# A two-layer decoder trunk: seven products for the second MLP matrix, woven with the first matrix, on weight sums that accumulating DMAs form

## The chip, the cores and the metric

The kernel runs on one core of one Trainium2 chip. The metric is the device time of one execution in microseconds (us), less is better. Before the change three runs gave 2387.39, 2388.78 and 2389.77 us; the median is 2388.78.

## The reference, cut to what matters

The trunk has two layers on a sequence of 1024 tokens of width 1024. Layer 0 mixes tokens by sliding-window attention beside a gated delta rule (the hybrid stage), layer 1 by a recurrent block. After each mixer comes a layer norm, then an MLP with squared ReLU, then another layer norm. The MLP is what the change touches:

```python
def sqrelu_mlp(x, w1, w2):          # x (1024, 1024), w1 (1024, 4096), w2 (4096, 1024)
    h = jax.nn.relu(x @ w1)
    return (h * h) @ w2
...
    x = layer_norm(DN_ALPHA * x + mix, ln1_g[layer], ln1_b[layer])
    x = layer_norm(DN_ALPHA * x + sqrelu_mlp(x, mlp_w1[layer], mlp_w2[layer]), ln2_g[layer], ln2_b[layer])
```

## The kernel before, in words

**Two chunks, two streams.** The 1024 tokens are cut into two chunks of 512. Each chunk is a Python generator, `stream(c)`: hybrid stage, output projection and layer norm (`mix_out`), MLP and layer norm (`mlp_ln`), four recurrent blocks (`rec_block`), output projection and layer norm, MLP and layer norm. A driver loop at the end of `trunk` decides at each step which stream (or which of the small generators in `mixers`: attention, delta rule, layer norms) puts its next instructions on the tensor engine. A stream yields nothing after a product inside a unit, `UNIT` at the end of a unit, `BLOCK` when it has to wait (for tiles of a ring, or for a flag). The stream with the lower `phase` goes first (0 in a mixer stage, 1 in the MLP of layer 0, 2 in that of layer 1), and of two in the same phase chunk 0; a stream that is in its recurrent blocks (`light`) gives the other one a turn after each unit. So the MLP of one chunk fills the gaps of the other chunk's mixer. The `Clock` class is a rough model of the engines; it only serves to choose this order. The tensor engine's instructions are then chained in the order of issue (`_pe`). On the other engines and queues a scheduler orders the instructions, and can move them ahead of earlier-written ones when their operands are there.

**Precision.** Every large product is done in three (`mm3`, L204 in the profile is the matmul call): high part by high part, high by low, low by high; high and low are float32r tiles that add up to the float32 one. Weights come by DMA in blocks of 128 x 1024 floats, 512 KB, on SP's queue into `ws` (`wblock`); the high part `wh` is a cast on ScalarE (ACT; on VectorE, DVE, every fifth time), the low part `wl = ws - wh` a subtraction on GpSimd (POOL) or DVE in turn, each for half a block, 512 columns. In the profile all of these have the line of a helper, L177; L207 is the transpose call.

**The MLP** (`mlp`). 4096 hidden rows are done in eight steps `e` of 512. In each, four blocks of the first matrix give hidden tiles of 128 rows x 512 tokens (8 x 3 = 24 matmuls of 512 columns each, `proj_fm`); ACT applies ReLU and squares, POOL squares again in full precision, DVE forms the low part. Then four blocks of the second matrix (2 output halves x 2) follow, 24 matmuls each, and for each of 4 token tiles and 2 halves DVE adds the bank to `yg`. So one step `e` is 192 matmuls, a pair of steps 384, and one chunk of one layer 1536. The last step of the last chunk of layer 1 is written so that the outputs come token tile by token tile, for the last layer norm to begin early.

**Order around the change.** Rings of SBUF tiles limit what is in flight: `g` (14 tiles of 128 x 2048), `t` (11), `s` (9), `f` (4) of 512 columns; `ws` 3 blocks; `wh` and `wl` 4 half-blocks each; PSUM has 4 banks `mm` and 4 banks `mx`. Chunk 0's MLP of layer 0 runs beside chunk 1's hybrid stage; chunk 0 then waits until chunk 1's first layer norm is written before its recurrent blocks, which alternate unit by unit with chunk 1's MLP; chunk 1's recurrent blocks wait for chunk 0's second output projection and alternate with chunk 0's MLP of layer 1; chunk 1's MLP of layer 1 comes last.

Of the kernel before, what the change touches and what calls it, by code (L numbers as in the profile page):

```python
# [17 lines left out]
P = 128  # L18
D = 1024
# [8 lines left out]
WB, HV, LG = 4, 5, 2  # L28
RINGS = dict(t=11, s=9, f=4)
# [29 lines left out]
class Clock:  # L59
    """Orders the tensor engine's work by a rough model of the engines: when each product's operands will be there."""  # L60
# [103 lines left out]
    def engine(self, eng, key):  # L164
        clk = self

        class Engine:
            def __getattr__(self, op):
                f = getattr(eng, op)

                def call(*a, **k):
# [6 lines left out]
                    if op == "dma_start":  # L178
                        clk.issue("D", outs, ins, max(0.06, aps[0].nbytes() / 360e3), 0.0, 2.0)
                        return r  # L180
# [20 lines left out]
    def matmul(self, out, lhsT, rhs, start, stop):  # L201
        n = int(np.prod(rhs.shape[1:]))
        c = 0.00042 * n * (1 if rhs.dtype == F32R else 4) if lhsT.shape[-1] > 32 else 0.046
        return self._pe(self.pe.matmul(out, lhsT, rhs, start=start, stop=stop), out, [lhsT, rhs], c, start)  # L204
# [6 lines left out]
def trunk(ctx: ExitStack, tc, I, out):  # L211
# [3 lines left out]
    DS, DA = clk.engine(nc.sync, "V"), clk.engine(nc.scalar, "V")  # L215
# [32 lines left out]
    def tl(r, dt=F32):  # L248
        return take(r, tpool.tile([P, 516], dt, tag=r, name=nm(r), bufs=RINGS[r]))

# [88 lines left out]
    def wblock(src, n=1024, hl=None):  # L339
        st = clk.tile("ws", 3, wpool.tile([P, 1024], F32, tag="ws", name=nm("ws"), bufs=3))[:, :n]  # L340
        DS.dma_start(st, src)
        m = n // 2
        if hl is None:
            hl = [clk.tile(t, WB, wpool.tile([P, 512], F32R, tag=t, name=nm(t), bufs=WB))[:, :m] for _ in range(2) for t in ("wh", "wl")]
        for i in range(2):
            h, l = hl[2 * i:2 * i + 2]
            a = st[:, i * m:(i + 1) * m]
            wcount[0] += 1
            if wcount[0] % HV == 0:
                V.tensor_copy(h, a)  # L350
            else:
                S.copy(h, a)
            if wcount[0] % LG == 0:
                G.tensor_tensor(l, a, h, ALU.subtract)
            else:
                V.tensor_tensor(l, a, h, ALU.subtract)
        return ([hl[0], hl[2]], [hl[1], hl[3]])

    def mm3(ps, lh, ll, rh, rl, start, stop):
        PE.matmul(ps, lh, rh, start=start, stop=False)  # L360
        PE.matmul(ps, lh, rl, start=False, stop=False)
        PE.matmul(ps, ll, rh, start=False, stop=stop)
# [34 lines left out]
    def load_xT(c, x, k2):  # L397
# [5 lines left out]
        else:  # L403
            st = clk.tile("ws", 3, wpool.tile([P, 1024], F32, tag="ws", name=nm("ws"), bufs=3))[:, :1024]
# [7 lines left out]
    def proj_fm(src, x, bank=None):  # L412
        wh, wl = wblock(src)
# [86 lines left out]
    def mlp(layer, yT, yg, ls, res=None):  # L500
        w1, w2 = I[f"w1_{layer}"], I[f"w2_{layer}"]
        for e in range(8):
            sh, sl = [], []
            yield from need("s", 9)
            wb, own = [], []
            if e == 7 and res is not None:
                yield from need("g", 4)
                for b in range(4):
                    t = gran(F32R)
                    own.append(t)  # L510
                    wb.append(wblock(w2[e * 4 + b], hl=[t[:, i * 512:(i + 1) * 512] for i in range(4)]))
            for f in range(4):
                ps = yield from proj_fm(w1[e * 4 + f], yT)
                h, l, r = ts("s", F32R), ts("s", F32R), ts("s")
# [4 lines left out]
                free("s", r)  # L519
                sh.append(h)  # L520
                sl.append(l)
                if e == 7 and f == 3:
                    yT.free()
# [812 lines left out]
```

## Time and profile before

| what | value |
|---|---|
| runs | 2387.39, 2388.78, 2389.77 us |
| span of the profiled execution | 2384.5 us; no time beside the span is recorded for that execution |
| mean granted TensorE clock | 0.992 |
| TensorE (PE) matmuls, busy | 12724, 2298.9 us, 96% |
| DVE, ACT, POOL busy | 56%, 38%, 35% |
| moved by DMA | 227.43 MB, 95 GB/s in the mean |

The span runs from the first to the last instruction of the profiled execution, and is 4.3 us below the median of the runs. PE's row counts a matmul as busy until its modelled end, so what it does is better read from the number of matmuls in a stretch that it fills. In names such as `mm<-g,wh` the first is the tile written, the others are read: `mm<-g,wh` and `mm<-g,wl` are products of the first MLP matrix (activations in `g`), `mm<-wh,s` and `mm<-wl,s` those of the second (hidden tiles in `s`). `ws<-w` are loads of MLP weights, `ws<-rin`, `rg`, `rout` of the recurrent block's, `ws<-hin...`, `hout` of the hybrid stage's.

### The profile page before, as it was taken

To read this page: it belongs to the slowest core of one execution; us is meant where nothing else is said; L and a number is where in the kernel's file an instruction comes from. 1 tells how busy PE (TensorE), PEld (TensorE's weight loads), DVE (VectorE), ACT (ScalarE), POOL (GpSimd) and SP (SyncE) were. 2 spreads that over 40 slices of the span, in tenths; PEclk is the share of its full clock that TensorE was granted. 3 is DMA by queue.
4 is the path that set the end of the run, shared out by engine and by line. 5 is a ranking of instruction groups with operands and counts; after the bars stand their busy time and mean duration, and the time that the engine had idled before them with its cause. 6 is when DMAs were issued, how large, how long until landed. Compare 5 with 4: busy or idle time off the path is not lost. (4 is left out here: it accounts for less than half of the span.)

```text
span 2384.5 us, 33354 instructions
## 1 busy us (share of the span) xinstructions
PE 2298.9 (96%) x12724; PEld 1841.9 (77%) x12724; DVE 1345.1 (56%) x2550; ACT 912.7 (38%) x1813; POOL 843.0 (35%) x706
## 2 busy tenths in 40 slices
PE   8889997999999999999999999999999999999997
PEld 7666775677777878778887788877887788778876
DVE  7697659565754463755664623565665543633345
ACT  5364424443333242454443322344554232322331
POOL 3342334232332243433443432343333333433341
PEclk9999998999999999999999999999999999999999
DMA  4121231122233222322333222232325222332231
GB/s 154 54 81 31 81 124 36 54 69 74 73 114 110 95 88 98 123 89 97 98 131 125 82 96 97 97 121 91 98 93 177 85 97 97 107 115 98 98 117 51
DMA packets 67487, 227.43 MB, mean 95 GB/s; under 512 B 7424, under 2 KB 7808, under 8 KB 67328
## 3 DMA queue, kind: packets, MB, share of 16 engines
q1 hardware_dynamic: 58832, 204.01, 25.9%
q10 hardware_dynamic: 8496, 21.30, 2.5%
q8 instruction: 100, 1.64, 0.3%
q14 instruction: 59, 0.48, 0.1%
HBM read 216.89 MB, written 8.39 MB: 94 GB/s over the span
## 5 line engine op out<-in xcount | busy, mean ns | idle before, releaser
L177 POOL TENSOR_TENSOR wl<-ws,wh 128x512 fp32r<-128x512 f32 (+1 forms) x372 | 497.6, 1338 | 1261.4 <-ACT wh L177 979.4
L204 PE MATMUL mm<-g,wh 128*128 128x512 f32 x2816 | 886.7, 396 | 0.5 <-DVE g L177 0.5
L177 ACT CAST wh<-ws 128x512 fp32r<-128x512 f32 (+1 forms) x595 | 365.5, 616 | 993.0 <-PE mm L204 910.1
L204 PE MATMUL mm<-wh,s 128*128 128x512 f32 x1984 | 648.2, 399 | 11.4 <-ACT s L177 5.7
L204 PEld LDWEIGHTS mm<-g,wh 128*128 128x128 f32 x2816 | 520.2, 189 | 107.2 <-issue 2.9
L204 PE MATMUL mm<-g,wl 128*128 128x512 f32 x1408 | 550.9, 391 | 5.4 <-POOL wl L177 5.4
L204 PEld LDWEIGHTS mm<-wh,s 128*128 128x128 f32 x1984 | 374.0, 189 | 102.6 <-ACT s L177 6.2
L204 PE MATMUL mm<-wl,s 128*128 128x512 f32 x992 | 391.9, 395 | 2.3 <-POOL wl L177 1.4
L177 DVE TENSOR_TENSOR wl<-ws,wh 128x512 fp32r<-128x512 f32 (+1 forms) x372 | 281.2, 756 | 188.8 <-ACT wh L177 184.4
L204 PEld LDWEIGHTS mm<-g,wl 128*128 128x128 f32 x1408 | 265.1, 188 | 64.0 <-POOL wl L177 7.1
L204 PE MATMUL mm<-wh,g 128*128 128x512 f32 (+1 forms) x768 | 235.2, 380 | 10.0 <-ACT wh L177 6.1
L177 DVE TENSOR_TENSOR s<-s,s 128x512 fp32r<-128x512 f32 x128 | 100.4, 784 | 242.9 <-POOL s L177 231.1
L204 PEld LDWEIGHTS mm<-wl,s 128*128 128x128 f32 x992 | 187.4, 189 | 43.3 <-POOL wl L177 1.8
L177 DVE TENSOR_TENSOR g<-g,mm 128x512 f32<-128x512 f32 x224 | 144.0, 680 | 130.7 <-PE mm L204 130.5
L204 PEld LDWEIGHTS mm<-wh,g 128*128 128x128 f32 x768 | 142.0, 190 | 38.7 <-ACT wh L177 6.1
L177 DVE CAST wh<-ws 128x512 fp32r<-128x512 f32 (+1 forms) x149 | 73.8, 495 | 172.6 <-PE mm L204 165.0
L177 POOL TENSOR_TENSOR s<-s 128x512 f32<-128x512 f32 x128 | 145.3, 1135 | 26.4 <-ACT s L177 26.4
L204 PE MATMUL mm<-wl,g 128*128 128x512 f32 (+1 forms) x384 | 143.7, 374 | 0.1
L177 ACT ACTIVATE s<-mm 128x512 f32<-128x512 f32 x128 | 75.9, 593 | 62.1 <-PE mm L204 61.9
L177 ACT ACTIVATE s<-s 128x512 fp32r<-128x512 f32 (+1 forms) x136 | 83.5, 614 | 19.0 <-DVE s L177 8.0
L204 PEld LDWEIGHTS mm<-wl,g 128*128 128x128 f32 x384 | 72.9, 190 | 11.9 <-DVE wl L177 0.4
L204 PE MATMUL mx<-g,wh 128*128 128x512 f32 x256 | 78.8, 389 | 0.0
(209 smaller groups left out, 2230.3 us busy)
## 6 DMA issues: line engine op xcount, KB each, us to landing
ws<-w SPq DMA_DIRECT2D x256, 512.0 KB, 3.3
ws<-hin_fm SPq DMA_DIRECT2D x32, 512.0 KB, 3.3
ws<-rin SPq DMA_DIRECT2D x32, 512.0 KB, 3.3
ws<-hout SPq DMA_DIRECT2D x16, 512.0 KB, 3.4
ws<-rout SPq DMA_DIRECT2D x16, 512.0 KB, 3.4
t<-ln ACTq DMA_DIRECT2D x28, 256.0 KB, 4.2
ws<-hin_q SPq DMA_DIRECT2D x8, 512.0 KB, 3.2
g<-x ACTq DMA_DIRECT2D x8, 512.0 KB, 5.0
```

Of the source, the lines that this page charges most:

```text
L177: r = f(*a, **k)
L204: return self._pe(self.pe.matmul(out, lhsT, rhs, start=start, stop=stop), out, [lhsT, rhs], c, start)
```

## The change

**Seven products.** A pair of steps (1024 hidden rows, index `j` = 0 to 3) multiplies a 512 x 1024 by a 1024 x 1024 matrix. The change cuts both into quarters, `a11 .. a22` (256 tokens x 512 hidden rows) and `b11 .. b22` (512 x 512), and forms the four output quarters from seven products instead of eight (the Strassen-Winograd form). Each product is 2 weight blocks of 12 matmuls, a unit each, so a pair takes 168 matmuls for the second matrix instead of 192. Four of the products need sums of weight quarters (`t1` to `t4`), and three need sums of hidden quarters, which DVE forms in place, 128 x 1024 at a time (four such instructions a pair). The hidden tiles are kept in float32 in `g` tiles, and each unit makes its own split of them (an ACT copy and a DVE subtraction of 512 columns) into two tiles of the ring `s` or `t`. Products accumulate on in a bank after DVE has added it to `yg` (`more=True` in `mm3`): two banks `mm` and two `mx` stay taken. DVE adds a bank to `yg` 14 times a pair instead of 16. In this path every `wl` is formed on DVE (`pool=False`).

**Where it is used.** `mlp` goes through plain steps (`straight`) until a check at an even step succeeds: chunk 1, or chunk 0 once chunk 1's output projection of the same layer is done (`op`). From there on `first(j)` makes the hidden tiles of a pair, and `weave` alternates one unit of `first(j + 1)` (24 matmuls) with two units of `seven(j)` (12 each); the last `seven` of a chunk has no partner. The last chunk of layer 1 starts with one plain step and closes with the old token-by-token step (`ends`, `finish`), so that it has three pairs.

**Weight sums.** `w2_sums` writes `t1` to `t4` of 2 layers x 4 pairs to DRAM. For each pair: four copies of 1 MB on SP's queue, 4 us of the model's clock apart; seven accumulating DMAs of 1 MB on POOL's queue in rows of 8 KB, 5 us apart; 8 us more, then the pair counts as summed, and `seven` may begin. A scheduling edge keeps each one behind the tensor engine's last instruction at that point. It starts when chunk 1's hybrid stage is over.

**Order.** Chunk 1's first layer norm in each layer waits until chunk 0 has used up the first matrix of that layer (`m7`); chunk 0's second layer norm of layer 0 waits for chunk 1's `m7`; a recurrent block `b` of chunk 1 waits for block `b` of chunk 0, no longer for its output projection. Chunk 1's recurrent blocks use ring `s`.

**Tiles.** Ring `s` 10 instead of 9, its square helper in a ring of its own (`r`, 2); `wh`, `wl` 3 whole blocks each instead of 4 half-blocks; the split works on a whole block, 1024 columns, at a time.

```diff
-WB, HV, LG = 4, 5, 2
-RINGS = dict(t=11, s=9, f=4)
+WB, WS, HV, LG = 3, 3, 5, 2
+RINGS = dict(t=11, s=10, f=4)
...
+    def split(h, l, x, key):
+        wcount[0] += 1
+        (V.tensor_copy if wcount[0] % HV == 0 else S.copy)(h, x)
+        (G if key else V).tensor_tensor(l, x, h, ALU.subtract)
...
+    def w2_sums():
...
+        for layer, j in ((i, j) for i in range(2) for j in range(4)):
+            for k, (first, *_) in SUMS.items():
+                behind(DS.dma_start(rows(tsum[layer][j][k]), rows(w2_quarter(layer, j, first))))
+                t = clk.now + 4.0
+                yield lambda: t
+            for i in range(1, 4):
+                for k, v in SUMS.items():
+                    if i < len(v):
+                        t = clk.now + 5.0
+                        yield lambda: t
+                        behind(DG.dma_start(rows(tsum[layer][j][k]), rows(w2_quarter(layer, j, v[i])), accum_op=ALU.add,
+                                            max_dma_last_dim=8192))
+            summed.add((layer, j))
+            t = clk.now + 8.0
+            yield lambda: t
...
+        def hidden(f, z):
+            ps = yield from proj_fm(w1[f], yT, mm_ps, False)
+            used()
+            S.activation(z, ps, AF.Relu)
+            S.activation(z, z, AF.Square)
+            yield UNIT
+
+        def seven(j, g, done):
...
+            yield from wait(lambda: (layer, j) in summed)
+            A = {f"a{r + 1}{q + 1}": v4(g[q])[:, :, r * 256:(r + 1) * 256] for q in range(2) for r in range(2)}
+            bank = {}
+            for i, (a, b, acc, out, sign, last) in enumerate((
+                    ("a12", "b21", "R", (0, 0), 1, False), ("a11", "b11", "X", (0, 0), 1, True),
+                    ("a21", "t1", "R", (1, 1), 1, False), ("a21", "t2", "X", (0, 1), -1, False),
+                    ("a12", "b22", "R", (0, 1), 1, True), ("a21", "t3", "X", (1, 1), -1, True),
+                    ("a22", "t4", "X", (1, 0), 1, True))):
...
+                for p in range(2):
+                    yield from wait(lambda: either(2))
+                    ring = either(2)
+                    ah, al = ts(ring, F32R), ts(ring, F32R)
...
+                    S.copy(ah2, x)
+                    V.tensor_tensor(al2, x, ah2, ALU.subtract)
+                    wh, wl = wblock(w2_quarter(layer, j, b)[p * P:(p + 1) * P], pool=False)
+                    for k in range(2):
+                        for t in range(2):
+                            mm3(bank[acc][t], ah2[:, k, t * P:(t + 1) * P], al2[:, k, t * P:(t + 1) * P], wh[k], wl[k],
+                                start and p + k == 0, p + k == 2, not start)
+                            if p + k == 2:
+                                accumulate(bank[acc][t], 2 * out[0] + t, out[1], sign, done and last)
...
+        if res is not None:
+            yield from straight(6, False)
+        while e < 8 and not ((c == 1 or sts[1].get("op", -1) >= layer) and rings["g"] >= 2 and e % 2 == 0):
+            yield from straight(e, e == 7)
+            e += 1
+        if e < 8:
+            n = 3 if res is not None else 4
+            yield from first(e // 2)
+            for j in range(e // 2, n):
+                nxt = first(j + 1) if j + 1 < n else ends() if res is not None else None
+                yield from weave(nxt, seven(j, hids.pop(j), j == 3), 2)
+        if res is not None:
+            yield from finish()
```

290 lines of the change are left out of this document (183 added, 107 removed).

## The prediction, made before the changed kernel ran

> **What bounds the kernel now.** I read the page's busy shares first, then the busy time by stretches, then single matmuls in the timeline, then the groups of the other engines, and last the queue of weight loads.
>
> ```profile
> span 2384.5 us, 33354 instructions
> PE 2298.9 (96%) x12724; PEld 1841.9 (77%) x12724; DVE 1345.1 (56%) x2550; ACT 912.7 (38%) x1813; POOL 843.0 (35%) x706
> ```
>
> ```profile
> 500.00:2325.00 1825.00, 1799.15 (x8811) 1460.78 (x8811) 942.21 (x1537) 682.79 (x1194) 654.87 (x531) 1.00 0.31 102
> ```
>
> The second fence is the stretch from the middle of the hybrid stage to the last hidden blocks (columns: us, then PE, PEld, DVE, ACT, POOL, then granted clock, DMA share, GB/s). PE idles 1825 - 1799 = 26 us there and the clock is 1.00: matmuls are what it waits for, and a matmul less is time less, as long as nothing new stops PE. The other engines have room in the mean: DVE, the fullest, is busy 942 of 1825 us.
>
> **Part 1: fewer matmuls.** What one costs, from the timeline of PE (start, length, names):
>
> ```profile
> 2252.14 0.62 PE L204 MATMUL mm<-g,wh 128*128 128x512 f32 x2
> ...
> 2258.94 0.62 PE L204 MATMUL mm<-g,wh 128*128 128x512 f32 x2
> ...
> 2260.08 0.64 PE L204 MATMUL mm<-wh,s 128*128 128x512 f32 x2
> ...
> 2280.25 0.63 PE L204 MATMUL mm<-wh,s 128*128 128x512 f32 x2
> ```
>
> The first two rows are 10 groups of three apart (30 products of the first matrix in 6.80 us, 227 ns each), the last two 29 groups (87 of the second matrix in 20.17 us, 231.8 ns each). A pair of steps does 168 instead of 192: 24 x 0.2318 = 5.56 us saved per pair.
>
> A page has a price for this too: the Trainium skill, "TensorE: Matmul & The Clock Gate", section "Wait — 56ns, not 53.3ns?", gives 215.7 ns from start to start for 512 columns once warm, by which a pair would save 5.18 us; the row above is the kernel's own and stands.
>
> How many pairs? Chunk 1 has four in layer 0 and three in layer 1 whatever happens. Chunk 0 has those that begin after chunk 1's output projection. From SP's queue:
>
> ```profile
> 350.97 120.62 SPq L177 DMA_DIRECT2D ws<-w  x11
> ...
> 661.85 93.06 SPq L177 DMA_DIRECT2D ws<-w  x14
> 761.25 40.03 SPq L177 DMA_DIRECT2D ws<-hout  x8
> 806.39 165.26 SPq L177 DMA_DIRECT2D ws<-w  x30
> ...
> 1555.88 0.33 SPq L177 DMA_DIRECT2D ws<-rin  x1
> ...
> 1807.83 5.56 SPq L177 DMA_DIRECT2D ws<-w  x2
> 1818.67 41.01 SPq L177 DMA_DIRECT2D ws<-rout  x8
> ```
>
> Before `hout` of chunk 1 (761 us), 40 blocks `ws<-w` were issued (the first 11 and the last 14 shown): eight a step, so five steps. If the order up to there stays, chunk 0 does step 5 plainly, and the check at step 6 succeeds: one pair. In layer 1, 28 blocks (3.5 steps) go between the first `rin` of chunk 1 and its `rout` (first and last shown). In the new order some of chunk 1's recurrent units pass under chunk 0's projection and norm, so I put chunk 0 at step 2 to 3 when chunk 1's projection begins; the check at step 4 succeeds: two pairs. Sum 1 + 4 + 2 + 3 = 10 pairs, 240 matmuls, **-55.6 us**; from 7 pairs (-39) to 11 (-61).
>
> **Part 2: the other engines under the seven products.** One unit of `seven` is 12 matmuls, 12 x 0.2318 = 2.78 us of PE. What it asks of DVE goes by these rows:
>
> ```profile
> 2225.48 0.68 DVE L177 TENSOR_TENSOR wl<-ws,wh 128x512 fp32r<-128x512 f32 x1
> 2226.09 1.87 DVE L177 TENSOR_TENSOR g<-g,mm 128x512 f32<-128x512 f32 x3
> 2229.73 0.43 DVE L177 CAST wh<-ws 128x512 fp32r<-128x512 f32 x1 [1.77 <-PE mm L204]
> ```
>
> Back to back, a 512-column DVE instruction takes 2226.09 - 2225.48 = 0.61 us. A unit has: a hidden split 0.61, `wl` of a whole block 1.22, one bank added 0.61, a fourteenth of the four 1024-column sums of hidden quarters 4 x 1.22 / 14 = 0.35, and a fifth of a cast of 2 x 0.43 us, 0.17: 2.96 us. Alone, `seven` is thus held by DVE by 0.18 us a unit, 2.5 us over its 14 units, 39 us of PE. Woven, two units go with a hidden block of 24 x 0.227 = 5.44 us of PE and 1.4 us of DVE: 7.3 of 11.0 us, no bound. `seven` stands alone at the end of chunk 0's part in each layer and of chunk 1's in layer 0, where a layer norm also wants DVE: **+7**, from 0 (DVE works ahead in the tiles of two rings) to 20. Removing POOL's 8 squares a pair and its `wl` is worth nothing: the weights are split ahead of PE. ACT has 0.62 + 2 x 0.62 = 1.9 us a unit by this row, under 2.78:
>
> ```profile
> L177 ACT CAST wh<-ws 128x512 fp32r<-128x512 f32 x582 | 360.5, 620 | 991.1 <-PE mm L204 908.4 <-PE mx L204 51.8 <-issue 20.7
> ```
>
> **Part 3: layer norms that change their cover.** Chunk 1's first layer norm now waits until chunk 0 has used its first matrix. Rows of ACT, PE and DVE around it today:
>
> ```profile
> 756.18 0.96 ACTq L177 DMA_DIRECT2D t<-ln  x2
> ```
>
> ```profile
> 774.97 0.60 PE L207 MATMUL mx<-csb,t 128*128 128x128 f32 x4
> ```
>
> ```profile
> 825.76 0.39 PE L204 MATMUL mm<-wh,g 128*128 128x512 f32 x1
> ```
>
> ```profile
> 829.71 0.70 DVE L177 SCALAR_TENSOR_TENSOR g<-g,lnw,t 128x512 f32<-128x512 f32 x1
> ...
> 859.71 0.68 DVE L177 TENSOR_TENSOR g<-mx,g 128x512 fp32r<-128x512 f32 x1
> ```
>
> From the first normalisation to the last split it is 30 us. PE ends the output projection at 826; step 5 is 4 x 5.44 + 4 x 5.56 = 44 us, and `first(3)` 8 x 5.44 = 43.5: the flag comes at about 913. The sums begin when the hybrid stage is over, at 775 (second row), and a pair takes 4 x 4 + 7 x 5 + 8 = 59 us, with about 0.5 more at each of 12 steps 65; pair 3, chunk 0's only one, is summed at 775 + 4 x 65 = 1035. So between 913 and the norm's end PE has nothing to put under it. The first row shows that work goes out ahead of its place in the program (the norm's loads go 74 us before the norm). If its arithmetic does too, it is over before 913, and only transposes and the last splits stand open: +3. If not, +30. I take **+3**.
>
> Chunk 0's recurrent blocks now run against chunk 1's last `seven` and then against chunk 1's own second norm, in place of a long MLP. `seven` has 14 units; alternating they last 14 x (5.44 + 2.78) = 115 us, then the norm takes 30, and chunk 0 has 20 units, about 6 left, 33 us: just enough. **+5**, from 0 to 30.
>
> **Part 4: the sums' transfers.** There is no accumulating DMA in this trace. The price of 1 MB:
>
> ```profile
> q1 hardware_dynamic: 58832, 204.01, 25.9%
> ```
>
> ```profile
> ws<-w SPq DMA_DIRECT2D x256, 512.0 KB, 3.3
> ```
>
> ```profile
> 1044.00:1165.00 121.00, 118.90 (x520) 97.08 (x519) 73.33 (x92) 62.21 (x101) 46.36 (x44) 1.00 0.29 96
> ```
>
> 204 MB took 25.9% of 16 engines' 2384.5 us, so 330 GB/s at full use, and 1.05 MB is 3.2 us of all engines. An accumulation costs between that (as a copy) and three times that, 9.6 us (source and destination read, then written, each at that rate). I take 5: nearer to the copy's row, since reading and writing already overlap in a copy. A pair then needs 4 x 3.2 + 7 x 5 = 48 us of the engines, and weights at the 29% of the last row take 19 of each 65: 67, full but in step. Weights land in 3.3 us today. Woven, 22 blocks in 82 us leave three block buffers 11.2 us, less 2.5 for the split: 8.7 us to land; a copy of 3.2 to 6.4 us ahead of a load in the same SP queue makes 6.5 to 9.7. So PE waits at few of them: **+8**, from 0 to 30. POOL issues seven transfers in 65 us; SP's issue of a load takes 0.33 us, a POOL issue was never seen here; POOL is 65% idle and splits weights ahead of PE, so even several us each, and a wait of t4's third accumulation for its second (5.5 us later), cost nothing until POOL falls a block of 5.5 us behind. Whole-block splits and three block buffers of `wh` in place of two change the hybrid stage by 0, plus or minus 5.
>
> Sum: -55.6 + 7 + 3 + 5 + 8 = -32.6. The span would be 2352; with the 4.3 us between span and median of the runs, 2388.8 - 32.6 = **2356 us**.
>
> **The rivals.** (a) **The sums come late** (slower). PE's order is fixed when the kernel is built, by the clock of a model; chunk 0's pair 3 stands in it at 1035 whether its sums are there or not. The last of the sums, t4, is used 12 units (33 us) in, which with the 8 us of grace gives about 36 us for all. At 6.4 us an accumulation, a pair needs 12.8 + 45 + 19 = 77 of 65 us, 12 late a pair, 48 after four: 12 us of standstill. At 8.5 us it is 26 a pair, 104 after four: 68 us, and 2388.8 - 32.6 + 68 = **2424**. It decides from 33 us of standstill on, about 7.3 us an accumulation. For: the accumulation must read its destination too. Against: DMA engines are 69% idle now. The Trainium skill, "DMA: Bandwidth & Descriptors", says in "Rules for kernel authors" that an accumulating DMA reads its destination and writes it later, and in "Bandwidth" that 1 MB issued from GpSimd takes 6.15 us; estimated by that for copies and sums alike, the fourth pair would be 4 x (68 + 19 - 65) = 88 us late and the time 2408. No trace here shows it.
>
> (b) **Cover lost**: the arithmetic of the norm is not done ahead, and the recurrent stages of two chunks against each other leave PE idle at both their ends: 27 + 25 us on top, 2388.8 - 32.6 + 52 = **2408**. For: 30 us of norm, and no long MLP beside chunk 0's recurrent blocks. Against: the early loads.
>
> (c) **Fewer pairs**: chunk 0's check fails in both layers, 7 pairs, -39 + 20: **2370**.
>
> (d) **Nothing gained**: short units make DVE and the weight loads the bound where `seven` runs, 0.4 us in each of 14 x 10 units takes back 56, all of part 1 in place of parts 2 to 4: **2388**. Against: DVE at 7.3 of 11 us when woven.
>
> **How the numbers follow.** Forecast 0.52, (c) 0.14, (d) 0.10, (a) 0.13, (b) 0.11. What a measurement can tell from no change is about 0.2%, 5 us. Of (d) I give 0.08 to no change; (a) and (b) are slower, with a little of (d): 0.25; the rest, 0.67, is faster. The range: all ten pairs and hardly a stall is 2388.8 - 54 = 2335; at the other end it takes in (b) at 2408 and the milder (a): 2410. The forecast's own range is 2335 to 2372.
>
> **What would show it.** Right: 12724 - 240 = 12484 matmuls or near, PE idle between 500 us and the last hidden blocks below 60 us, weight loads of 4 to 8 us while the sums run, and `seven` alone with DVE as the releaser. Wrong: PE waiting on a DMA of `t1` to `t4` near 1035 (a); 20 to 30 us of idle PE before chunk 1's first hidden block or after chunk 0's last recurrent block (b); about 12556 matmuls (c).

## The result, and the profile after

The changed kernel takes 2443.55 us (median of four runs, 2442.12 to 2446.47), the kernel before 2388.12 us beside it (2387.39 to 2389.77): a ratio of 1.0232, 95% interval 1.0220 to 1.0244. It is 55 us slower, and 34 us beyond the upper end of the range.

From the page after (the execution took 2442.44 us): the span, the busy times, DMA engines' busy tenths in 40 slices of 61 us, SP's and POOL's DMA queues with packets, MB and share of 16 engines' time, and POOL's issues of accumulating transfers. In the changed kernel the matmul call is L206, the helper L178 and the transpose call L210.

```profile
span 2440.7 us, 32068 instructions
...
PE 2264.4 (93%) x12460; PEld 1808.9 (74%) x12460; DVE 1551.8 (64%) x2537; ACT 1003.5 (41%) x1723; POOL 550.9 (23%) x399
...
DMA  4220231122235899979887862422443443534452
...
q1 hardware_dynamic: 69360, 272.17, 32.3%
q0 software_dynamic: 8064, 58.72, 11.9%
...
L178 POOL DMA_DIRECT2D t<-w x56 | 45.9, 866 | 373.5 <-DMA t<-w 359.7
...
t<-w POOLq DMA_DIRECT2D x56, 1024.0 KB, 12.0
```

PE does 12460 matmuls, 264 fewer: eleven pairs, one more than forecast, 264 x 0.2318 = 61 us less work. It spends more time all the same. The third row shows where to look: from the 14th slice to the 23rd the DMA engines are busy to seven to nine tenths, where two to four are usual elsewhere. The last rows are the new transfers: 56 accumulations took 11.9% of 16 engines' 2440.7 us, 290 us, so **5.2 us of all engines each** (forecast 5), but each lands 12.0 us after its issue, and POOL stands 360 us waiting for earlier ones before it may issue the next.

The stretch that the prediction's second fence showed, up to the last hidden blocks, which come some 60 us later now, and four parts of it (us; PE, PEld, DVE, ACT, POOL; clock, DMA share, GB/s), after:

```profile
500.00:2385.00 1885.00, 1770.71 (x8564) 1431.46 (x8563) 1148.47 (x1556) 777.89 (x1150) 374.37 (x260) 0.97 0.54 166
...
767.00:1000.00 233.00, 223.69 (x983) 183.34 (x982) 108.21 (x132) 75.16 (x103) 47.92 (x40) 0.98 0.89 250
1000.00:1320.00 320.00, 277.94 (x1110) 216.11 (x1109) 186.88 (x234) 114.64 (x155) 28.62 (x30) 0.94 0.88 257
1320.00:1420.00 100.00, 92.61 (x409) 74.25 (x408) 80.63 (x88) 54.70 (x79) 42.10 (x31) 0.98 0.83 236
1420.00:1700.00 280.00, 239.69 (x1049) 194.93 (x1048) 208.50 (x253) 159.03 (x228) 101.77 (x67) 0.94 0.33 109
```

Three of these parts before:

```profile
767.00:1000.00 233.00, 229.44 (x1033) 187.13 (x1032) 126.89 (x207) 75.84 (x127) 88.04 (x67) 1.00 0.30 100
1000.00:1320.00 320.00, 316.70 (x1384) 259.03 (x1383) 178.18 (x237) 143.61 (x232) 115.29 (x103) 1.00 0.33 109
...
1420.00:1700.00 280.00, 275.45 (x1216) 224.84 (x1215) 138.40 (x209) 112.62 (x183) 99.98 (x81) 1.00 0.31 101
```

PE's idle time in the long stretch has grown from 26 to 114 us. The count of matmuls tells it best: from 1000 to 1320 us, where the units of `seven` are woven with the hidden blocks, PE does 1110 instead of 1384, 274 x 0.2318 = 64 us behind; from 1420 to 1700, where the transfers are over (DMA share 0.33), 167 behind, 39 us; from 767 to 1000, with just as much DMA traffic, only 50, 12 us. DVE, ACT and POOL are not near their limits: DVE, the fullest of them, has 187 of 320 us.

What the loads did from 1000 to 1320, after (count, KB each, median us from issue to landing):

```profile
t<-w POOLq DMA_DIRECT2D x25, 1024.0 KB, 12.1
ws<-w SPq DMA_DIRECT2D x43, 512.0 KB, 7.3
ws<-t SPq DMA_DIRECT2D x28, 512.0 KB, 8.9
t<-w SPq DMA_DIRECT2D x14, 13.4
```

Weight loads, of `w` and of the sums `t` alike, land in 7 to 9 us instead of 3.3. The view of waits in the same stretch shows who stood for them:

```profile
ACT wh L178 <- DMA ws<-t: 63.6, 13, 9.2
ACT wh L178 <- DMA ws<-w: 62.8, 15, 9.0
...
PE mm L206 <- ACT wh L178: 19.8, 11, 5.8
PE mm L206 <- DVE wl L178: 13.9, 18, 2.7
```

(In this view: us in total, times, longest wait.) ACT's cast waits 126 us for loads, PE for the cast and the low part 34. PE names ACT and DVE as releasers, but they are held up themselves; one step further back stands the DMA.

PE's waits do not make up the whole loss. Its idle time from 1000 to 1320 is 320 - 278 = 42 us, and the granted clock there is 0.94 instead of 1.00. Right after a wait the matmuls themselves are slower, as two rows of PE's timeline behind a wait of 2.07 us for `wh` show:

```profile
1107.90 1.05 PE L206 MATMUL mm<-wh,s 128*128 128x512 f32 x2
...
1109.18 1.05 PE L206 MATMUL mm<-wh,s 128*128 128x512 f32 x2
```

A group of three takes 1.28 us here, where the prediction's rows have 0.68 to 0.70 (3 x 0.227 and 3 x 0.2318). So a late load costs more than the wait that it causes.

And one wait after the transfers, in PE's timeline:

```profile
1471.42 2.82 PE L210 MATMUL mx<-csb,g 128*128 128x128 f32 x12 [23.75 <-DVE g L178]
```

These are the first transposes of chunk 1's second layer norm of layer 0. PE stood still for 23.75 us, and the units that follow in the fixed order were behind these transposes.

### The profile page after: what moved, and what is told of

The parts are those of the page before. It is cut to its first block, busy times and chain, and to the rows that moved or that the text cites. A ratio compares the mean times of both kernels' runs of the same rounds, so it can differ in the third digit from the quotient of the medians.

```text
span 2440.7 us, 32068 instructions
## 1 busy us (share of the span) xinstructions
PE 2264.4 (93%) x12460; PEld 1808.9 (74%) x12460; DVE 1551.8 (64%) x2537; ACT 1003.5 (41%) x1723; POOL 550.9 (23%) x399
## 3 DMA queue, kind: packets, MB, share of 16 engines
q0 software_dynamic: 8064, 58.72, 11.9%
## 4 chain that ended last, share of the span: by engine, by line
PE 63%; DVE 20%; DMA 7%; ACT 5%; issue 2%; POOL 0%; ACTq 0%; DVEq 0%; POOLq 0%
PE mm L206 50%; PE mx L206 11%; DVE g L178 7%; DMA ws<-w 6%; DVE wl L178 3%; DVE t L178 3%; DVE s L178 2%; ACT wh L178 1%; DVE lnw L178 1%; DVE f L178 1%; PE mx L210 1%; DVE hsc L178 1%; DMA ws<-t 1%; ACT t L178 1%; ACT g L178 1%
## 5 line engine op out<-in xcount | busy, mean ns | idle before, releaser
L206 PE MATMUL mm<-g,wh 128*128 128x512 f32 x2816 | 891.9, 398 | 10.9 <-ACT wh L178 7.2
L178 ACT CAST wh<-ws 128x1024 fp32r<-128x1024 f32 (+1 forms) x350 | 364.8, 1042 | 789.3 <-PE mm L206 595.1
L178 DVE TENSOR_TENSOR wl<-ws,wh 128x1024 fp32r<-128x1024 f32 (+1 forms) x335 | 420.6, 1257 | 393.0 <-ACT wh L178 388.9
L206 PEld LDWEIGHTS mm<-g,wh 128*128 128x128 f32 x2816 | 523.4, 190 | 122.9 <-ACT wh L178 9.6
L206 PE MATMUL mm<-g,wl 128*128 128x512 f32 x1408 | 554.1, 394 | 11.9 <-DVE wl L178 11.9
L178 POOL TENSOR_TENSOR wl<-ws,wh 128x1024 fp32r<-128x1024 f32 (+1 forms) x103 | 252.2, 2448 | 831.8 <-ACT wh L178 461.3
L206 PE MATMUL mm<-wh,s 128*128 128x512 f32 x1216 | 410.6, 405 | 26.7 <-ACT wh L178 12.6
L206 PEld LDWEIGHTS mm<-g,wl 128*128 128x128 f32 x1408 | 266.6, 189 | 73.5 <-DVE wl L178 16.7
L206 PEld LDWEIGHTS mm<-wh,s 128*128 128x128 f32 x1216 | 235.1, 193 | 82.4 <-ACT wh L178 15.7
L206 PE MATMUL mm<-wl,s 128*128 128x512 f32 x608 | 243.7, 401 | 9.3 <-DVE wl L178 9.3
L206 PE MATMUL mm<-wh,g 128*128 128x512 f32 (+1 forms) x768 | 231.6, 379 | 9.2 <-ACT wh L178 6.3
L206 PE MATMUL mx<-wh,s 128*128 128x512 f32 x528 | 171.0, 392 | 3.2 <-DVE s L178 1.7
L206 PEld LDWEIGHTS mm<-wh,g 128*128 128x128 f32 x768 | 142.5, 191 | 35.7 <-ACT wh L178 6.3
L206 PEld LDWEIGHTS mm<-wl,s 128*128 128x128 f32 x608 | 117.8, 194 | 36.0 <-DVE wl L178 13.0
L206 PE MATMUL mm<-wl,g 128*128 128x512 f32 (+1 forms) x384 | 143.9, 375 | 0.3 <-DVE wl L178 0.3
L178 ACT CAST s<-g 128x512 fp32r<-128x512 f32 x158 | 95.5, 620 | 99.3 <-PE mm L206 50.6
L178 DVE TENSOR_TENSOR s<-g,s 128x512 fp32r<-128x512 f32 x158 | 110.4, 713 | 36.0 <-ACT s L178 35.9
L178 POOL DMA_DIRECT2D t<-w x56 | 45.9, 866 | 373.5 <-DMA t<-w 359.7
L178 DVE CAST wh<-ws 128x1024 fp32r<-128x1024 f32 x88 | 62.3, 708 | 94.8 <-PE mm L206 60.2
L206 PEld LDWEIGHTS mx<-wh,s 128*128 128x128 f32 x528 | 99.0, 188 | 25.1 <-DVE s L178 3.0
L178 DVE TENSOR_TENSOR g<-g,mm 128x512 f32<-128x512 f32 x140 | 92.0, 681 | 28.5 <-PE mm L206 28.3
L206 PE MATMUL mx<-wl,s 128*128 128x512 f32 x264 | 103.3, 391 | 3.5 <-DVE wl L178 3.5
```

The costliest lines, as they stand in the source:

```text
L178: r = f(*a, **k)
L206: ins = self.pe.matmul(out, lhsT, rhs, start=start, stop=stop, skip_group_check=fresh)
```

## The experiments

Two theories stood against each other at first. **T**: the transfers of the sums take the bandwidth from the weight loads. **C**: cover is lost, above all under that norm. The further ones, with letters of their own, are in the expectations, which are quoted as they were put on record. The kernel before ran beside every group, with medians of 2387.46 to 2388.29 us. All kernels are the changed one with the edit shown, unless said otherwise. Runs 9 and 11 to 18 also carry a guard of two lines in the model's clock, which skips an entry that is no longer queued.

### 1. No traffic for the sums

```diff
-behind(DS.dma_start(rows(tsum[layer][j][k]), rows(w2_quarter(layer, j, first))))
-behind(DG.dma_start(rows(tsum[layer][j][k]), rows(w2_quarter(layer, j, v[i])), accum_op=ALU.add, ...))
+clk.issue("D", [...], [...], 2.9, 0.0, 2.0)     # both: the model's entry alone, so PE's order stays
...
-return tsum[layer][j][q] if q in SUMS else ...
+return ... the first quarter of the sum, as it lies in w2
```

> The changed kernel without the 32 copies and 56 accumulating DMAs: no sum is formed, each of t1 to t4 is read from the raw quarter that it would start from, so four of the seven products multiply by the wrong weights. The order of the tensor engine's instructions is the same, instruction for instruction. Theory T (the sums' transfers fill the DMA engines, 0.88 to 0.89 busy from 767 to 1320 us, and the weight loads land in 8 to 11 us and up to 24 instead of 3.3): the 80 us that PE loses in matmuls between 767 and 1420 us come back, 2443 - 75 = 2368 us, between 2355 and 2380, with the loss of 39 us between 1420 and 1700 still there. Rival D (short units, whole-block splits and all low parts on DVE make DVE late, and the transfers only look guilty): under 15 us come back, 2430. Rival L (the loss between 1420 and 1700 is itself an effect of the delay before it, since the order was planned by a clock that knows no delay): both come back, about 2330.

2373.12 us (2373.01 to 2376.14), ratio 0.9942 [0.9927, 0.9956]. Its windows and its wait:

```profile
767.00:1000.00 233.00, 227.48 (x1006) 186.64 (x1005) 109.57 (x136) 78.25 (x107) 33.39 (x18) 0.99 0.28 97
1000.00:1320.00 320.00, 309.25 (x1361) 253.35 (x1361) 234.81 (x288) 148.76 (x204) 27.37 (x17) 0.99 0.42 145
1320.00:1420.00 100.00, 74.52 (x333) 60.41 (x332) 82.34 (x103) 53.70 (x77) 40.32 (x29) 0.88 0.33 116
1420.00:1700.00 280.00, 265.54 (x1152) 216.86 (x1151) 187.25 (x218) 155.53 (x221) 98.92 (x61) 0.97 0.32 110
```

```profile
PE mx L210 <- DVE g L178: 34.3, 12, 24.1
```

With the same order of PE's work, the transfers cost 2443.6 - 2373.1 = 70 us, as T had it. The matmuls tell where: against this run the changed kernel is 23 behind from 767 to 1000, 251 from 1000 to 1320 and 27 from 1320 to 1700; these 301 x 0.2318 are 70 us. Of the 58 us in the middle part some 31 are idle time of PE (42 against 11) and the other 27 slower matmuls. The 24 us under the norm (last number of the last row) stay, so they are no effect of the traffic, C does not explain the 70, and rival L of the expectation is out. From 1320 to 1700 this run does 1485 matmuls against 1647 before, some 38 us behind, though it has no transfers: that part of the loss belongs to the order of the work. The rows say something more: without sums the woven stretch asks for 0.42 of the DMA engines by itself, the plain one before it for 0.28.

### 2. Plain products, the rest of the change kept

```diff
-            spawn(w2_sums())
...
-        while e < 8 and not ((c == 1 or sts[1].get("op", -1) >= layer) and ...):
+        while e < (8 if res is None else 6):
...
```

> The changed kernel with all products of the second matrix done plainly, eight and not seven, and no sums: what is left of the change is the order of the two chunks, the rings, the whole-block splits and three block buffers. Against the run without the sums' traffic it has 264 matmuls more, 61 us. If order and splits cost nothing of themselves: 2388. Theory H (the new order of the chunks leaves the layer norm of chunk 1 and the recurrent blocks uncovered, some 39 us): 2425. Rival S (it is the DVE work of seven beside chunk 0's recurrent blocks that opens that gap, since DVE was 90% busy there): 2390 to 2400.

2421.87 us (2418.75 to 2424.45), 1.0142 [1.0127, 1.0157]. That is close to theory H's 2425. So the seven products alone are worth 2421.9 - 2373.1 = 49 us of the 61 that their matmuls come to, and the order of the chunks, the rings and the buffers cost 34 us against before.

### 3. Layer 1's sums later, and 4. all sums earlier

```diff
+            if layer:                                      # run 3
+                yield from wait(lambda: "m7" in sts[1])
...
-        if c == 1:                                         # run 4
+        if c == 0:
             spawn(w2_sums())
```

> The sums of layer 0 as they are, those of layer 1 only from the moment when chunk 1 has used up the first matrix of layer 0, about 1320 us, into the recurrent blocks, whose own traffic is low. Theory T: from 1100 to 1320 us the loads land early again, about 45 us back there, and a little lost after 1320: 2400, between 2390 and 2410. Rival D: 2435 to 2445.

> The sums begin when chunk 0's hybrid stage is over, about 290 us, instead of chunk 1's: they are through at about 930. The engines for DMA are 20 to 30% busy there, and weights are read in blocks of 5.4 us or more, not of 2.78. Theory T: of 80 us some 50 come back; but POOL waits for one accumulation before it issues the next on the same sum, and in the hybrid stage POOL has work that the delta rule's chain needs, which costs 10 to 25: 2400 to 2420. Rival D: 2440, or slower by POOL's waits.

Run 3: 2404.7 us (2398.48 to 2406.77), 1.0074 [1.0057, 1.0090], as T had it: half of the transfers, moved out of the woven stretch, give back 39 us. Run 4: **2373.81 us** (2372.02 to 2375.42), 0.9941 [0.9926, 0.9956], below every range that was expected (the 10 to 25 us of POOL's waits did not come), and 14 us faster than the kernel before. It moves the same bytes as the changed kernel and, in an order of PE's work of its own, takes no longer than run 1 without transfers. Its windows:

```profile
500.00:767.00 267.00, 262.84 (x2062) 207.38 (x2061) 148.59 (x307) 93.70 (x208) 103.03 (x83) 1.00 0.90 242
...
1000.00:1320.00 320.00, 315.97 (x1405) 260.37 (x1405) 209.14 (x237) 149.70 (x208) 19.85 (x12) 1.00 0.40 138
```

Before, the first of these stretches had:

```profile
500.00:767.00 267.00, 263.88 (x2064) 208.06 (x2064) 151.26 (x340) 98.67 (x238) 84.54 (x75) 1.00 0.27 90
```

At 0.90 of the DMA engines PE does 2062 matmuls where it did 2064 at 0.27: beside the hybrid stage the transfers are free. The granted clock is 1.00 here, so the transfers do not lower it by themselves; in the changed kernel it is low where PE had waited. A full DMA system is no harm by itself. It harms where the loads that share it are needed at once. The changed kernel shows the same from 767 to 1000 us:

```profile
ws<-w SPq DMA_DIRECT2D x34, 512.0 KB, 8.1
```

The loads land as late there as in the woven stretch, and only 5 us are lost: a plain block lasts PE 24 matmuls, 5.5 us, a block of `seven` 2.8.

### 5. Cover for the norm, and 6. low parts on POOL again (both on run 4's kernel)

```diff
-        yield from mlp_ln(0, c, s, "t", False)             # run 5
+        yield from mlp_ln(0, c, s, "ts"[c], False)
...
-                    wh, wl = wblock(..., pool=False)       # run 6, and proj_fm in hidden
+                    wh, wl = wblock(...)
```

> The sums early as in the run before, and chunk 1's layer norm after the MLP of layer 0 takes its four tiles of gains and offsets from ring s, not t. Theory R: the 24 us in which PE waits for that norm at about 1375 us come from ring t: the norm holds four of its eleven tiles, chunk 0's last recurrent block needs them, is blocked, and so four hidden blocks of 5.4 us and the gates' 5.5 that could lie under the norm are planned behind it. Then 15 to 25 us come back: 2352, between 2347 and 2362. Rival V: DVE is too busy there for any order to help: 2368 to 2376.

> The sums early, and the low parts of the weights formed on POOL and DVE in turn in the woven part too, as in the plain steps, instead of on DVE alone (the order of the tensor engine's instructions stays, instruction for instruction). Theory V (where seven meets recurrent blocks and norms, DVE at 80 to 95% is the bound): 5 to 15 us come back, 2362. Rival: these waits are for single results, not for DVE's throughput, and POOL's 2.4 us for a block come later than DVE's 1.2: 2370 to 2378.

Both missed. Run 5: 2384.57 us (2378.62 to 2390.49), 0.9988 [0.9976, 0.9999], 11 slower than run 4. The 24 us are gone (such waits come to 9 in all, the longest 1.9), and others have come:

```profile
PE mx L206 <- DVE t L178: 19.4, 12, 10.2
PE mx L206 <- ACT t L178: 13.8, 5, 6.6
PE mm L206 <- ACT r L178: 10.8, 4, 5.9
...
PE mx L210 <- issue: 9.0, 2, 8.5
```

Its 12484 matmuls are ten pairs: the ring changed the order, and chunk 0 began its seven products one pair later. 5.6 us are that pair; the other 5 may be that the work put under the norm was needed elsewhere, but they are no more than small edits move this kernel by (runs 13 to 18). Run 6: 2383.9 us (2381.5 to 2387.6), 0.9979 [0.9970, 0.9988], with DVE relieved by 87 us in all (1475.8 busy instead of 1562.4) and 10 us slower. Theory V's 2362 is out. A low part of a block takes POOL 2.4 us and DVE 1.3 (means on the changed kernel's page), so a relief of DVE came together with later low parts, and the run does not weigh the two apart.

### 7. Copies on ACT's queue, and 8. copies without accumulations

```diff
-behind(DS.dma_start(rows(tsum...                           # run 7
+behind(DA.dma_start(rows(tsum...
...
-behind(DG.dma_start(..., accum_op=ALU.add, ...))           # run 8
+clk.issue("D", [...], [...], 2.9, 0.0, 2.0)
```

> The changed kernel with the 32 copies issued from ACT's queue instead of SP's; nothing else. Theory Q (loads are late because a copy of 1 MB stands in front of them in SP's own queue): over 25 of the 70 us that the traffic costs come back, 2400 to 2418. Theory F (the 16 engines are full and the loads share them, whichever queue the copies are in): under 10 us, 2433 to 2446.

> The changed kernel with the 32 copies and without the 56 accumulations: t1 to t4 stay what the copy put there, so four of the seven products multiply by the wrong weights. The order on PE is the same. The accumulations took 11.9% of 16 engines' span, 290 us or 5.2 us each, the copies about 2 to 3 each. Theory F: nearly all of the 70 us come back, 2375 to 2385. Theory Q: about half, 2405.

Run 7: 2452.25 us (2449.78 to 2453.34), 1.0264 [1.0249, 1.0279]: 9 slower than the changed kernel, outside both ranges. That a copy stands ahead of a load in SP's queue is not the cost. The Trainium skill, "DMA: Bandwidth & Descriptors", section "Issuing engines are not separate DMA queues", says that all of them run on the same 16 engines whoever starts them; this run agrees, with a DMA share of 0.86 from 1000 to 1320 us where the changed kernel had 0.88. Run 8: 2378.46 us (2375.63 to 2381.94), 0.9957 [0.9942, 0.9973]: of the 70 us the 32 copies cost 5, the 56 accumulations 65. Its woven stretch:

```profile
1000.00:1320.00 320.00, 309.09 (x1363) 252.81 (x1362) 235.46 (x289) 149.37 (x205) 27.95 (x17) 0.99 0.57 205
```

The copies add 0.15 to the 0.42 of run 1, and PE does 1363 matmuls, as without them (1361). Whether the accumulations do their harm by their share alone or also by their kind or the queue that they come from is open: no run filled the engines as far with plain copies.

### 9. The old order, with seven products in layer 1 only, and 10. the old order with plain products

```diff
-"s" if c == 0 else "t", s, st[c]["t"], lambda: c == 0 or "m7" in sts[0])
+"s" if c == 0 else "t", s, st[c]["t"], lambda: True)
+st[c]["ln1"] = True
...
+        if c == 0:
+            yield from wait(lambda: "ln1" in st[1])
+        else:
+            yield from wait(lambda: "rec" in st[0])
...
-            yield from wait(lambda: c == 0 or sts[0].get("rb", 0) > b)
-                yield from rec_block(c, b, s["x"], hT, s, "ts"[c])
+                yield from rec_block(c, b, s["x"], hT, s, "t")
...
-                if c == 0:
-                    yield from wait(lambda: "m7" in sts[1])
...
+        while e < 8 and not (layer and ...        # run 9; layer 1's sums alone, 15 us apart
...                                               # run 10: plain products, as in run 2
```

> The order of the two chunks as it was before the change (chunk 0's recurrent blocks beside chunk 1's MLP, chunk 1's beside chunk 0's), rings and whole-block splits as changed, and seven products only in layer 1, where the rings have room: four pairs, 96 matmuls, 22 us less. The sums of layer 1 alone, begun after chunk 1's hybrid stage, accumulations 15 us apart. Theory H (what is left of the loss without traffic, some 34 to 46 us, lies in the new order, which puts the two recurrent stages against each other with no long MLP beside them): 2370, between 2362 and 2378, faster than before by about 0.8%. Rival D (it lies in the splits and in seven itself): 2385 or more.

> The changed kernel's rings, whole-block splits and three block buffers of high and low parts with the old order of the chunks, plain products only and no sums: 12724 matmuls as before. Theory H: within 5 us of before, 2383 to 2393, and so the new order costs 2422 minus this, about 34 us. Rival D: 2400 or more, the splits cost it.

Run 10 (run 2 with the old order): 2405.97 us (2403.8 to 2408.52), 1.0074 [1.0058, 1.0089], so of the 34 us of run 2 the new order is 16, and 18 stay in a kernel that has no sums, no seven products and the old order. Theory H, which had put all of it on the order, missed here and by 3 us in run 9. Run 9, four pairs in layer 1 beside it: 2380.87 us (2378.98 to 2383.75), 0.9972 [0.9961, 0.9984], 25 under run 10; its 96 fewer matmuls come to 22. So here, with the sums spread out, the seven products seem worth all that they save. The two kernels differ in PE's order, though, and runs 13 and 14 will show plain products in the old order at 2390, with one other edit each, only 9 above run 9.

### 11 and 12. Half-block splits again, in run 10's kernel and in run 4's

```diff
+        m = x.shape[1] // 2
+        for i in range(2):
+            hi, li, xi = (z[:, i * m:(i + 1) * m] for z in (h, l, x))
...
```

> As the run with the old order and plain products, but each weight block split in two halves of 512 columns again, cast and low part, on three whole-block buffers. Theory G (the 18 us that rings and splits cost come from instructions of 1024 columns standing in front of short ones of the norms and chains on ACT, DVE and POOL): 2386 to 2394. Rival (they come from the rings and from what the planner then does around the norms): 2400 to 2410.

> The changed kernel with the sums begun early, which ran at 2374, and each weight block split in two halves again. Theory G: 10 to 18 us less, 2356 to 2364, the best of all. Rival: 2370 to 2380, since the woven part has more instructions on DVE.

2411.92 us (2409.55 to 2414.98), 1.0096 [1.0081, 1.0112], and 2375.81 us (2373.24 to 2377.82), 0.9949 [0.9936, 0.9961]: 6 slower than run 10, the same as run 4. Theory G is out: the splits' size is not the 18 us.

### 13 to 16. The rings and the buffers

```diff
-either = lambda n: next((r for r in "st" if rings[r] >= n), None)   # run 13, on run 10's kernel
+either = lambda n: "s" if rings["s"] >= n else None
...
-WB, WS, HV, LG = 3, 3, 5, 2                                         # run 14, on run 10's; run 16, on run 4's
+WB, WS, HV, LG = 2, 3, 5, 2
...
-r = clk.tile("r", 2, ...)                                           # run 15: 13 and 14 and this
+r = ts("s")                                                         # with ring s = 9
```

> The kernel with the old order of the chunks and plain products only (2406.0 us, 18 above before), with one edit: a plain step takes its hidden tiles from ring s alone, as before the change, and no longer from ring t where s is short. Theory R (the +18 is rings: the MLP's steps take eight of the eleven t tiles that the recurrent blocks beside it need): about 2392, and the matrix engine's waits for DVE's additions (38 us in that kernel, 3 us before) mostly gone. Theory W (the +18 is split work done too far ahead: three whole blocks of wh and wl in place of two, so that DVE makes the low parts of later blocks first and is late with the additions that free the banks): 2404 to 2408, no change. Theory S (spread over several small edits): 2398 to 2404.

> The same kernel (2406.0 us) with one other edit: two whole blocks of wh and wl instead of three, the size of the buffers before the change. Theory W: about 2393, and the waits for DVE's additions mostly gone. Theory R: 2406 or slower, since the splits have less room ahead. Theory S: 2398 to 2404.

> The same kernel (2406.0 us) with both of these edits and the square helper back in ring s (9 tiles). What is left of the change then are whole-block splits (no loss by themselves: halves were 6 us slower), the layout of the second matrix in quarters and the code that makes all eight tiles of a step at its start. Theories R, W and S alike: within 5 us of before, 2385 to 2393. If it stays at 2400 or above, none of the rings and buffers is the cause.

> The changed kernel with the weight sums begun after chunk 0's hybrid stage (2373.8 us), with two whole blocks of wh and wl instead of three. Theory W, if it holds where the seven products are too: 2358 to 2368. Theory R: 2374 to 2385, slower, since a unit of the seven products uses up a block in 2.8 us and two blocks leave less ahead.

Run 13: 2389.62 us (2386.01 to 2393.52), 1.0007 [0.9998, 1.0017]. Run 14: 2390.37 us (2384.46 to 2392.35), 1.0008 [0.9998, 1.0018]. Run 15: 2386.97 us (2384.73 to 2390.39), 0.9999 [0.9989, 1.0008]. Either edit alone gives the 16 us back, so they are not a sum of two costs, and neither theory is right as it was put. The largest wait of PE for DVE in run 10 and in run 13:

```profile
PE mm L206 <- DVE g L178: 38.3, 12, 8.7
```

```profile
PE mx L212 <- DVE g L180: 25.7, 10, 5.8
...
PE mm L208 <- DVE g L180: 6.2, 4, 2.1
```

(The lines of runs 13 to 16 stand two further down; L212 there is the transpose call.) In run 10 matmuls wait for DVE to clear their bank into `yg`; in run 13 that wait has shrunk, and transposes wait more. In run 14, as fast as run 13, it is still 29.7 us:

```profile
PE mm L208 <- DVE g L180: 29.7, 13, 7.9
```

So this wait is not the 16 us either. Run 16: 2416.19 us (2415.39 to 2422.08), 1.0123 [1.0108, 1.0138]: with two split blocks the kernel of run 4 loses 42 us, more than either theory gave it. PE's largest wait for low parts there:

```profile
PE mm L208 <- DVE wl L180: 25.0, 26, 5.6
```

In run 4 this wait was 5.1 us. A unit of `seven` uses up a block in 2.8 us, and the seven products need the third buffer: 42 us are well above what the other edits of buffers did.

### 17 and 18. Ring t kept out of the plain steps, in run 4's kernel and in run 2's

```diff
-            yield from wait(lambda: either(8))
-            ring = either(8)
+            yield from need("s", 8)
+            ring = "s"
```

> The changed kernel with the weight sums begun after chunk 0's hybrid stage (2373.8 us), and a plain step that takes its tiles from ring s alone (a unit of the seven products may still use both rings). If the 16 us that this edit gave back in the old order are a cost of ring t as such, they come back here too: about 2358. If they belong to the order that the planner made of that kernel only, there is no reason for a gain: 2368 to 2382, of either sign, since only the few plain steps of chunk 0 and the last chunk's first step are touched.

> The kernel with the new order and plain products only (2421.9 us), with the same edit. If ring t costs 16 us whatever the order: 2406, and the new order costs 16 by itself. If the two overlap, so that the new order already pays for what ring t costs, 2415 to 2422. If the planner's orders scatter by this much under any small edit, anything from 2400 to 2430.

2380.24 us (2377.61 to 2382.6), 0.9968 [0.9954, 0.9982], and 2415.25 us (2412.9 to 2419.47), 1.0115 [1.0100, 1.0130]: one 6 us slower, the other 7 faster than its partner. The edit that gave 16 us in the old order has no fixed price. Run 18 fits two of its theories, that of the overlap and that of the scatter. Taken together, small edits of rings and buffers reorder the planned work, and the times here lie some 6 to 18 us apart without a cause that these runs name.

## Why the prediction was wrong, point by point

**The sum.** By the medians, from before: +34 (run 2: order, rings, buffers), -49 (seven products, run 2 to run 1), +70 (transfers, run 1 to the change) make the 55 us.

**Part 4, the step that failed.** It said of a pair "67, full but in step" and "So PE waits at few of them: **+8**, from 0 to 30". It was 70. The price of an accumulation came out, 5.2 us of all engines for 5. No row had spoken for 5 between the bounds of 3.2 and 9.6, so that was luck; an accumulation of 7.3 us, from which rival (a) was to decide, was not needed. What failed is the room, in two terms. I took the weights' own share, 29%, from a stretch of plain steps; the woven stretch asks for 0.42 (run 1). The prediction had the numbers for it: it counts 22 blocks in 82 us when woven, and at its 3.2 us for 1 MB, 1.6 a block, these are 35 of 82 us, 0.43. And a pair does not come every 65 us: in run 8, where nothing slows PE much, the first copies of the pairs are 73 us apart in the mean (eight pairs, first copies at 770 to 1279 us). With both put right a pair needs 48 + 0.42 x 73 = 79 of 73 us.

The engines were not full all the time either: in stretches of 20 us from 1000 to 1320 their share went from 0.54 to 1.07, for 0.88 in the mean. The transfers come in bursts; between two pairs POOL issues none for some 30 us (1049 to 1082, say). An estimate from three rows: sums that find room take 0.90 - 0.27 = 0.63 of the engines (run 4, 500 to 767), with the 0.42 that is 1.05, and at 0.88 everything would take 1.05 / 0.88 = 1.19 times as long; 1361 / 1.19 = 1144 matmuls from 1000 to 1320, measured 1110. The plain stretch asks for 0.28 + 0.63 = 0.91, and lost 23 matmuls to run 1, against 251. So the same transfers cost 5 us in one stretch and 58 in the next. The other side of the sum, the time for a load to land, was forecast at 6.5 to 9.7 us against 8.7 available; the medians were 7.3 and 8.9. Forecast and bound lay within one another, which should have been read as a coin's toss and not as "in step". Whether too little share or too little time for each load is the better account of the harm, these runs do not tell. Nor was it a price to be paid once: each transfer is held behind a PE instruction and each accumulation behind earlier ones, so sums and PE slowed down together, and by the same measure the pairs came 82 us apart.

**Rival (a)** had the resource right and the place wrong: no fourth pair stood still for its `t4`; weight loads of all kinds in the woven stretch were late. In the whole run only POOL waits for a `t<-w` (360 us, before its next accumulation); SP's queue never holds a load of `t` for an unfinished sum. Its 2424 was reached and passed.

**Part 1.** Right, and one pair better: 264 matmuls for 240, -61 for -55.6. Rival (c), seven pairs, is out.

**Part 2.** +7 forecast, 61 - 49 = 12 measured. The named cause, DVE's throughput in `seven` alone, is not shown: relieving DVE did not help (run 6), but made its low parts later. Rival (d), all of part 1 taken back, is out.

**Part 3.** For the first norm, +3: run 1 does 27 matmuls fewer than before from 767 to 1000, 6 us. For chunk 0's recurrent blocks against chunk 1's second norm, +5 of a range 0 to 30: there stands the wait of 24 us. I had counted six units left at that point, "just enough"; as I read the planned order, chunk 0's next recurrent block had no tiles left in ring t to start on, and with tiles from ring s for the norm the wait is indeed gone (run 5). The time did not gain, so the ring is not all of it. In all, the new order costs 2421.9 - 2406.0 = 16 us by one pair of kernels and 2415.3 - 2389.6 = 26 by another, for the 8 forecast. That is rival (b), in part; since 16 to 26 us are hardly more than the scatter of the orders, the size is uncertain.

**Part 4's "0, plus or minus 5"** for splits and buffers: 18 us in run 10, nothing in runs 13 to 15. Shown is that undoing either ring t for plain steps or the third block gives it back; that this is a scatter of the planned orders, and no mechanism of its own, is what runs 17 and 18 suggest. It is not settled: no run here holds PE's order fixed and changes a ring.

**What would have been right.** With the sums begun after chunk 0's hybrid stage the same change gives 2373.8 us, 14 faster than before: -61 + 12 + 34 and next to nothing for the transfers. That lies inside the forecast range, but the -61 and the 46 against it are not the forecast's -55.6 and 15.

## What to carry to other kernels

Price a background transfer in the stretch where it will run, by the share of the DMA engines that this stretch will ask for after the change, not by that of its neighbour today; here a sum of 0.90 to 0.91 cost nothing or 5 us, and one of about 1.05 cost 58. Count how many blocks the changed loop will load in a microsecond, since units of half the matmuls load more for the same work (here 22 blocks a pair in place of 16). Move such traffic to where loads have slack (here under the other mixer, where 0.90 cost nothing) before trimming it. And where an order is planned at build time, compare variants in pairs that differ in one thing, and treat 6 to 18 us as the scatter of orders until a second pair agrees.

## What the runs showed of the hardware

An accumulating DMA of 1 MB from DRAM to DRAM in 8 KB rows took 5.2 us of all 16 engines; it landed in a median of 10.0 us (run 4, 300 to 767 us) to 12.1 us (changed kernel, 1000 to 1320). POOL's issue of one took 0.82 us (45.9 us for 56). A copy of 1 MB landed in 7.9 us where no accumulation ran beside it (run 8) and in 13.4 in the changed kernel from 1000 to 1320. Over stretches of 200 us and more that were full of sums, the DMA engines' mean share was 0.86 to 0.90, with 235 to 257 GB/s moved. Loads of 512 KB then took 5.1 us beside the hybrid stage and 7 to 9 beside plain steps and the woven part, for 3.3 undisturbed. Behind waits of PE of a microsecond or two, matmuls of 512 columns came 0.43 us apart instead of 0.23 (1107.90 to 1109.18).

```profile
t<-w POOLq DMA_DIRECT2D x42, 1024.0 KB, 10.0
ws<-w SPq DMA_DIRECT2D x38, 512.0 KB, 5.1
```

These two rows are from the kernel with the early sums, 300 to 767 us.
